# A pinned order for the prologue of a fused transformer layer: row sums among the products of the quarter before, context rows last, extra products in the waits

## The chip, the cores and the metric

The kernel runs on one core of a Trainium2 chip. The number that counts is the device time of one execution in microseconds (us): the median before the change is 1426.35 us over three runs (1426.13, 1426.35 and 1907.31). The names of the engines are those of the profile: PE multiplies matrices, PEld loads its stationary operands, DVE works elementwise and reduces, ACT evaluates functions and copies, POOL is the slow general engine, SP issues the transfers (DMA). TensorE is another name of PE.

## The reference

One layer of a diffusion backbone, in float32: 1024 latent tokens and 256 context tokens of 1024 features. The part that the change touches is the beginning:

```
m_lat = silu(c) @ w_mod + b_mod           # shift and scale of the latent rows
m_ctx = silu(c_ctx) @ w_mod + b_mod       # the same for the context rows
h_lat = rms_norm(x, norm1_g) * (1 + sc1) + sh1
h_ctx = rms_norm(ctx, norm1_g) * (1 + csc1) + csh1
p = h @ w_in                              # 3584 columns, here the 512 of the retention values
```

Behind it come retention and differential attention on the seven column blocks of `w_in`, an output projection, a gated MLP with a depthwise convolution, and a final norm. The change leaves their code alone.

## The kernel before, in words

**Exactness.** Each float32 operand `a` is split into a part `hi`, rounded to a short float format, and the rest `lo = a - hi`. Every product is made in three passes (`passes`, lines 126 to 131): `hi*hi` at line 129, `hi*lo` at line 130, `lo*hi` at line 131, of 128x128 by 128x512 each. A slice of weights is loaded into `raw` (line 186), ACT casts it to `whi` (line 190) and DVE subtracts to `wlo` (line 191).

**The prologue.** It ends where the products `pl` of the next column block begin. The 1024 features are eight slices `d` (or `k`) of 128, taken in four quarters `q` of two slices each. The 1024 latent rows are eight tiles `t` of 128, in two halves. The work is this:

- *Row sums and columns* (`modulation1(q)`, lines 509 to 529). For a quarter, two tiles `wt` of 1 MB of `w_mod` are loaded, and eight products `pr` (line 516) sum them up with `silu(c)`. ACT copies the result to `rw` (line 520), four tiny products `pm` (line 523) turn it into columns, and three small DVE operations (lines 527 and 529) make shift and scale `mcol` of the two slices.
- *First half* (`raw_latents`, lines 566 to 584). A row tile `xt` is squared and summed by ACT (line 533). DVE (line 114) and POOL (line 115) make the factor of its norm, DVE scales the tile (line 535), eight PE transposes `px` (line 579) turn it, and ACT and DVE copy it into `xraw` (lines 582 and 584). `first_latents(q)` applies `mcol` to the two slices of the quarter: DVE at line 589, ACT casts `hi` (line 590), and POOL or DVE subtracts `lo` (line 592, POOL for the odd slice). Then it multiplies the slices with the weights into four running sums `part`, printed as `pn`, one for each row tile.
- *Context rows and second half* (`context_rows`, `latents`). The rows are normed as above, and `modulate` (lines 537 to 548) turns a slice of all of them at once (`pt`, line 541) and makes its `hi` (ACT, line 544), `tmp` (DVE, line 546) and `lo` (line 548, POOL for odd slices). Then come the products of the context's two tiles, `cT`, and of the second half's four tiles, by `natural`.

The value tiles are evacuated by `store_to` (lines 400 to 409), centred and stored.

**What sets the order.** The work is written as generators: `beside(g, rate)` runs a generator next to another loop, which calls `tick()` and so lets the generator go on at that rate. The list of each engine is then set by a scheduler with a model of its own, which moves an instruction ahead of others that wait for operands. Each engine works down its list in order and waits on semaphores. `in_order(start)` ties neighbours of an engine's instructions from a point on in the order in which they are written; before the change it is used only at the end of the kernel. SP issues all loads of the prologue from one queue, in order. The tiles `wt` have four buffers, `xt` five, the weights' `raw` two, and the turned tiles `px`, `pt` and `pm` share three PSUM buffers.

Of the kernel before, what the change touches and what calls it, by code (L numbers as in the profile page):

```python
# [8 lines left out]
F32 = mybir.dt.float32  # L9
# [8 lines left out]
P = 128  # L18
# [42 lines left out]
TAIL = 2  # L61
EARLY = ("S1", "M1", "S0", "M0", "E1", "E0", "R", "C")
# [10 lines left out]
def kernel(  # L73
# [43 lines left out]
    def in_order(start):  # L117
        last = {}
        for ins in nc.cur_bb.bb.instructions[start:]:
            if ins.engine not in FORCE:  # L120
                continue
# [30 lines left out]
    with ExitStack() as p1:  # L152
# [3 lines left out]
        first = ExitStack()  # L156
        xr = first.enter_context(tc.tile_pool(name="xr", bufs=1, side="right"))
# [339 lines left out]
        with ExitStack() as p0:  # L497
# [11 lines left out]
            def modulation1(q):  # L509
                d0 = 2 * q  # L510
                pr = ps_b.tile([P, 512], F32, name="pr", tag="mm")
                for kk in range(2):
                    raw = xp.tile([P, 4, 512], F32, name="wt", bufs=4)
                    nc.sync.dma_start(out=raw, in_=w_mod[q][:, 4 * kk : 4 * kk + 4, :])
                    for j in range(4):
                        mm(pr[32 * j : 32 * j + 32, :], wide[:, 4 * kk + j, :], raw[:, j, :], start=(kk == 0), stop=(kk == 1), tile_position=(0, 32 * j), skip_group_check=True)
                    for j in range(4):
                        tick()
                rw = xp.tile([P, 512], F32, name="rw", bufs=1)
                nc.scalar.copy(rw, pr)  # L520
# [29 lines left out]
            def latents():  # L550
                xs = []
                for t in range(4, 8):
                    xt = xp.tile([P, D], F32, name="xt", bufs=5)
                    nc.sync.dma_start(out=xt, in_=x[t * P : (t + 1) * P, :])
                    normalize(xt, 2 + t)
                    xs.append(xt)
                    yield
                for d in range(KD):
                    modulate(xs, d, 0, hT[0][1][:, d, :], hT[1][1][:, d, :])
                    yield  # L560
# [5 lines left out]
            def raw_latents():  # L566
                xs = []
                for t in range(4):
                    xs.append(xp.tile([P, D], F32, name="xt", bufs=5))
                    nc.sync.dma_start(out=xs[t], in_=x[t * P : (t + 1) * P, :])  # L570
                yield
                for t, xt in enumerate(xs):
                    normalize(xt, 2 + t)
                    for g in range(2):
                        yield
# [915 lines left out]
```

## Time and profile before

| | |
|---|---|
| time, median of three runs | 1426.35 us |
| the profiled execution's own time | 1426.36 us |
| its span | 1424.6 us |
| PE busy | 1372.8 us, 96% of the span |
| first product `pr` of the prologue | 7.05 us |
| first product `pn` of the values | 24.58 us |
| first product `pl` of the next block | 107.72 us |

The profile page has busy times of each engine. A view by windows splits these into stretches of the span, and `PEclk` in it is the granted clock of PE (1.00 is full). The timeline lists one engine's instructions: start, the time from the first one's start to the last one's end, engine, line, operation, result and operands, count, and in brackets the idle time before them with what ended it. Matmuls overlap in it, so the step from one start to the next, and not the length printed, is what one costs. A float32 product that isn't split shows as two records.

### The profile page before, as it was taken

What the parts mean: (1) busy time and instruction counts of PE and PEld (TensorE: products, weight loads), DVE (VectorE), ACT (ScalarE), POOL (GpSimd) and SP (SyncE); (2) the same over time, 40 slices, a digit from 0 to 9 for tenths busy, and PEclk for the clock granted to TensorE, in tenths of its full rate; (3) what the DMA queues carried; (4) which work ended last, traced back from release to release, by engine and by line L of the source; (5) the groups of instructions that cost most, each with busy time, mean ns of one, the idle gap of its engine ahead of it and who ended that gap; (6) DMA issues with size and microseconds to landing.
All of it is one profiled execution on the core that took longest, in us unless ns stands there. A gap on an engine that the chain in (4) does not pass through costs nothing.

```text
span 1424.6 us, 19441 instructions
## 1 busy us (share of the span) xinstructions
PE 1372.8 (96%) x6924; PEld 1141.5 (80%) x6924; DVE 1009.1 (71%) x1503; ACT 735.3 (52%) x1402; POOL 358.9 (25%) x467
## 2 busy tenths in 40 slices
PE   6899999999999899999999999999999999999997
PEld 3578878878887789999888778888888888788886
DVE  3578855533467699888346897788877777898756
ACT  3535623212455688998225665445555545455433
POOL 1230000031777332421201133322222330034003
PEclk8999999999999999999999999999999999999999
DMA  8448874376458378461411223323322235953434
GB/s 321 172 151 303 297 257 144 126 250 189 138 174 203 123 184 184 107 130 60 163 67 74 84 86 112 108 99 111 111 91 82 102 111 177 386 209 107 134 97 148
DMA packets 106953, 219.87 MB, mean 154 GB/s; under 512 B 8868, under 2 KB 47268, under 8 KB 104936
## 3 DMA queue, kind: packets, MB, share of 16 engines
q1 hardware_dynamic: 98728, 193.72, 39.8%
q0 software_dynamic: 8128, 24.91, 7.9%
q8 instruction: 55, 0.90, 0.3%
q14 instruction: 42, 0.34, 0.1%
HBM read 161.18 MB, written 57.41 MB: 153 GB/s over the span
## 4 chain that ended last, share of the span: by engine, by line
PE 44%; issue 3%; DMA 2%; DVE 2%; ACT 1%; POOL 0%; POOLq 0%; DVEq 0%; ACTq 0%
PE chain L129 5%; PE chain L130 5%; PE chain L131 5%; PE c L131 4%; PE c L130 4%; PE c L129 4%; PE third L131 2%; PE third L130 2%; PE third L129 2%; PE po L131 2%; PE po L130 2%; PE po L129 2%; DMA W<-w_down 1%; PE second L130 1%; PE second L131 1%
## 5 line engine op out<-in xcount | busy, mean ns | idle before, releaser
L129 PE MATMUL chain<-T,whi 128*128 128x512 f32 x264 | 103.7, 393 | 5.9 <-ACT ub L1176 3.2
L129 PE MATMUL pl<-hT,whi 128*128 128x512 f32 x256 | 106.5, 416 | 0.0
L130 PE MATMUL chain<-T,whi 128*128 128x512 f32 x264 | 103.5, 392 | 0.0
L131 PE MATMUL chain<-T,wlo 128*128 128x512 f32 x264 | 103.2, 392 | 0.0
L131 PE MATMUL pl<-hT,wlo 128*128 128x512 f32 x256 | 100.6, 393 | 0.0
L130 PE MATMUL pl<-hT,whi 128*128 128x512 f32 x256 | 100.4, 392 | 0.0
L769 DVE TENSOR_REDUCE mt<-pA 128x1 f32<-128x1280 f32 x64 | 95.4, 1490 | 4.1 <-PE pA L766 3.6
L766 PE MATMUL pA<-ks,qhl 128*128 128x512 f32 (+1 forms) x384 | 89.5, 369 | 3.6 <-ACT p L773 3.6
L131 PE MATMUL c<-whi,ghl 128*128 128x512 f32 x232 | 90.4, 390 | 0.8 <-DVE ghl L1252 0.8
L1081 POOL TENSOR_TENSOR cmb<-wrb 128x512 f32<-128x512 f32 x20 | 27.3, 1363 | 250.8 <-DMA wrb<-w_up 156.9
L129 PE MATMUL c<-whi,ghl 128*128 128x512 f32 x232 | 90.3, 389 | 0.0
L130 PE MATMUL c<-wlo,ghl 128*128 128x512 f32 x232 | 90.3, 389 | 0.0
L129 PE MATMUL pn<-whi,hT 128*128 128x512 f32 x192 | 84.5, 441 | 3.7 <-ACT hT L590 3.7
L773 ACT ACTIVATE p<-pA,mt 128x1280 f32<-128x1280 f32 x64 | 85.4, 1335 | 2.4 <-DVE mt L769 2.4
L425 ACT ACTIVATE xb<-pl 32x512 f32<-32x512 f32 (+1 forms) x96 | 56.7, 590 | 52.9 <-PE pl L131 28.6
L932 ACT CAST whi<-cmb 128x512 fp32r<-128x512 f32 x62 | 38.6, 623 | 87.3 <-PE chain L130 65.3
L766 PEld LDWEIGHTS pA<-ks,qhl 128*128 128x128 f32 x384 | 67.6, 189 | 15.6 <-ACT p L773 4.3
L131 PE MATMUL pn<-whi,hT 128*128 128x512 f32 x192 | 76.4, 401 | 0.8 <-POOL hT L548 0.4
L798 PE MATMUL pv<-va,aT 128*128 128x128 f32 x640 | 77.0, 276 | 0.1
L130 PE MATMUL pn<-wlo,hT 128*128 128x512 f32 x192 | 77.0, 403 | 0.0
L798 PEld LDWEIGHTS pv<-va,aT 128*128 128x128 f32 x640 | 74.0, 192 | 0.7 <-DVE yT L827 0.3
L933 DVE TENSOR_TENSOR wlo<-cmb,whi 128x512 fp32r<-128x512 f32 x62 | 57.1, 924 | 21.9 <-ACT whi L932 21.9
(320 smaller groups left out, 3887.0 us busy)
## 6 DMA issues: line engine op xcount, KB each, us to landing
raw<-w_in SPq DMA_DIRECT2D x32, 512.0 KB, 4.8
wm<-w_mod SPq DMA_DIRECT2D x32, 512.0 KB, 4.7
wra<-w_up SPq DMA_DIRECT2D x24, 512.0 KB, 3.4
wrb<-w_up SPq DMA_DIRECT2D x23, 512.0 KB, 3.5
W<-w_down SPq DMA_DIRECT2D x44, 256.0 KB, 6.8
ad<-s SPq DMA_DIRECT2D x20, 512.0 KB, 3.5
wra<-ad SPq DMA_DIRECT2D x20, 512.0 KB, 3.4
wrb<-ad SPq DMA_DIRECT2D x18, 512.0 KB, 4.0
```

Of the source, the lines that this page charges most:

```text
L129: mm(ps, lh, rh, start=first, stop=False, skip_group_check=more)
L130: mm(ps, lh, rl, start=False, stop=False, skip_group_check=more)
L131: mm(ps, ll, rh, start=False, stop=last, skip_group_check=more)
L425: nc.scalar.activation(xb[q * blk : (q + 1) * blk, :], pt[o : o + blk, :], AF.Copy, scale=scale)
L766: mm(self.pa[m][:, c0:c1], self.q[:, i, m, qs], self.k[:, m, c0:c1], start=(i == 0), stop=(i == 1))
L769: nc.vector.tensor_reduce(out=self.mt[:, m : m + 1], in_=self.pa[m][:, :LK], axis=AX.X, op=ALU.min)
L773: nc.scalar.activation(self.p[m], self.pa[m][:, :LK], AF.Exp, scale=-1.0, bias=self.mt[:, m : m + 1], accum_out=self.s[:, m : m + 1])
L798: mm(self.pv, self.aT[:, c, :], self.v[:, c, :], start=(c == 0), stop=(c == NKT - 1))
L932: nc.scalar.copy(hi, src)
L933: nc.vector.tensor_tensor(out=lo, in0=src, in1=r32(hi), op=ALU.subtract)
L1081: nc.gpsimd.tensor_tensor(out=s1, in0=b1, in1=b2, op=ALU.add)
```

## The change

- All of the first half's loads go first: four `xt`, then `wt` of quarters 0 and 1 with a weight slice behind each pair. The rest follows as buffers come free: `wt` of quarter 2, a weight slice, the four row tiles of the second half, `wt` of quarter 3, a weight slice, the context rows.
- The order of PE and SP from there to the end of the first half's products is pinned as written, by `in_order` with those two engines. ACT, DVE and POOL stay with the scheduler.
- The row sums and columns of quarter `q` stand among the products of quarter `q-1`, and the features of quarter `q` are made while the rest of quarter `q-1` is multiplied.
- The second half is turned between the products of the last two quarters. Its products come next, and the context rows, turned between them, are multiplied last.
- `spare(n)` issues `n` products of a tile of ones with itself into a PSUM tile that nobody reads: 16 at the very start, 2 ahead of the first columns, 4 behind them.

The core of the diff (left out: the renaming of an ExitStack, and the moved bodies of functions that stay the same):

```diff
+SPARE = (16, 2, 4)
...
-    def in_order(start):
+    def in_order(start, engines=FORCE):
         last = {}
         for ins in nc.cur_bb.bb.instructions[start:]:
-            if ins.engine not in FORCE:
+            if ins.engine not in engines:
                 continue
...
-            def modulation1(q):
+            wts, prs = {}, {}
+
+            def weights(q, kk):
+                wts[q, kk] = xp.tile([P, 4, 512], F32, name="wt", bufs=4)
+                nc.sync.dma_start(out=wts[q, kk], in_=w_mod[q][:, 4 * kk : 4 * kk + 4, :])
+
+            def row_sums(q, kk):
+                if kk == 0:
+                    prs[q] = ps_b.tile([P, 512], F32, name="pr", tag="mm")
+                raw = wts.pop((q, kk))
+                for j in range(4):
+                    mm(prs[q][32 * j : 32 * j + 32, :], wide[:, 4 * kk + j, :], raw[:, j, :], start=(kk == 0), stop=(kk == 1), tile_position=(0, 32 * j), skip_group_check=True)
+
+            def columns(q):
                 d0 = 2 * q
...
+            def second_half():
+                rows = [xs[t] for t in range(4, 8)]
+                for t, xt in enumerate(rows):
+                    normalize(xt, 6 + t)
+                for d in range(KD):
+                    modulate(rows, d, 0, hT[0][1][:, d, :], hT[1][1][:, d, :])
+                    yield
+
+            def spare(n):
+                dm = pst.tile([P, 4, P], F32, name="dm", tag="tr")
+                for i in range(n):
+                    mm(dm[:, i % 4, :], ones, ones, start=True, stop=True)
...
-            beside(raw_latents(), 1.5, 1.0)
-            modulation1(0)
+            start = len(nc.cur_bb.bb.instructions)
+            for t in range(4):
+                row(t)
+            for q in range(2):
+                for kk in range(2):
+                    weights(q, kk)
+                more()
+            spare(SPARE[0])
+            raw_rows(0)
+            raw_rows(1)
+            row_sums(0, 0)
+            weights(2, 0)
+            raw_rows(2)
+            raw_rows(3)
+            row_sums(0, 1)
+            weights(2, 1)
             more()
+            for t in range(4, 8):
+                row(t)
+            spare(SPARE[1])
+            columns(0)
+            first_features(0)
+            spare(SPARE[2])
+
+            def values(q, n):
+                for _ in range(n):
+                    next(first[q], None)
+                    if q > 1 and turns[0] is not None:
+                        next(turns[0], None)
+
+            first, turns = [first_values(q) for q in range(4)], [None]
             for q in range(1, 4):
-                beside(first_latents(q - 1), 1.25, 0.0)
-                modulation1(q)
-                beside(iter(()), 0.0)
-                more()
-            todo = first_latents(3)
-            for _ in range(2):
-                next(todo)
-            beside(context_rows(), 1.5, 0.0)
-            for _ in todo:
-                tick()
-            beside(latents(), 0.75, 3.0)
+                values(q - 1, 3 if q == 1 else 1 if q == 2 else 2)
+                for kk in range(2):
+                    row_sums(q, kk)
+                    if q == 1:
+                        weights(3, kk)
+                if q == 1:
+                    more()
+                    xc = []
+                    for t in range(NTC):
+                        xc.append(xp.tile([P, D], F32, name=f"xc{t}"))
+                        nc.sync.dma_start(out=xc[t], in_=ctxt[t * P : (t + 1) * P, :])
+                values(q - 1, 1)
+                columns(q)
+                first_features(q)
+                if q == 3:
+                    turns[0] = second_half()
+                values(q - 1, 9)
+            values(3, 9)
+            for _ in turns[0]:
+                pass
+            in_order(start, (mybir.EngineType.PE, mybir.EngineType.SP))
+            beside(context_rows(), 0.4, 0.0)
+            natural(wget, lat_lhs, range(4, NT), keep_rv)
+            beside(iter(()), 0.0)
             natural(wget, ctx_lhs, range(NTC), store_to(kvg_row(1), center=True))
-            beside(iter(()), 0.0)
-            natural(wget, lat_lhs, range(4, NT), keep_rv)
```

`first_values(q)` yields after each of its eight products of three passes (a row tile and a slice), so `values(q, n)` writes `n` of them.

PE's list at the start of the program, before (px are the transposes of the first half's rows):

```order
L516 MATMUL pr<-wt,wide 32x512 x4
L579 MATMUL px<-ident,xt 128x128 x32
L516 MATMUL pr<-wt,wide 32x512 x4
L523 MATMUL pm<-fold,rw 128x2 x4
L129 MATMUL pn<-whi,hT_171 128x512 x2
L130 MATMUL pn<-wlo,hT_171 128x512 x2
L131 MATMUL pn<-whi,hT_173 128x512 x2
L516 MATMUL pr<-wt,wide 32x512 x4
```

and now (dm are the spare products, hT_171 and hT_173 the `hi` and `lo` of the first half's features):

```order
L607 MATMUL dm<-ones 128x128 x16
L573 MATMUL px<-ident,xt 128x128 x16
L521 MATMUL pr<-wt,wide 32x512 x4
L573 MATMUL px<-ident,xt 128x128 x16
L521 MATMUL pr<-wt,wide 32x512 x4
L607 MATMUL dm<-ones 128x128 x2
L529 MATMUL pm<-fold,rw 128x2 x4
L607 MATMUL dm<-ones 128x128 x4
L130 MATMUL pn<-whi,hT_171 128x512
L131 MATMUL pn<-wlo,hT_171 128x512
L132 MATMUL pn<-whi,hT_173 128x512
L130 MATMUL pn<-whi,hT_171 128x512
```

The first row sums have moved behind half of the transposes, the spare products stand at three places, and the products of the first quarter, which went two tiles at a time through one slice, go pass by pass through both slices of one tile.

SP's list from the start of the program, before:

```order
L514 DMA wt<-w_mod 128x2048
L570 DMA xt<-x 128x1024 x4
L514 DMA wt<-w_mod 128x2048
L186 DMA raw<-w_in 128x1024
L514 DMA wt<-w_mod 128x2048 x2
L186 DMA raw<-w_in 128x1024
L514 DMA wt<-w_mod 128x2048 x2
```

and now:

```order
L560 DMA xt<-x 128x1024 x4
L514 DMA wt<-w_mod 128x2048 x2
L187 DMA raw<-w_in 128x1024
L514 DMA wt<-w_mod 128x2048 x2
L187 DMA raw<-w_in 128x1024
L514 DMA wt<-w_mod 128x2048 x2
```

The first 1 MB of `w_mod` stands behind the four row tiles instead of ahead of them.

ACT's list around the third and fourth quarter, before (sq is the square of a row tile, xc a context tile, rw the copied row sums):

```order
L520 COPY rw<-pr 128x512
L190 CAST whi<-raw 128x1024
L590 CAST hT_171<-xraw 128x512 x2
L520 COPY rw<-pr 128x512
L190 CAST whi<-raw 128x1024
L533 ACTIVATE sq,sm<-xc_494 128x1024
```

and now:

```order
L526 COPY rw<-pr 128x512
L191 CAST whi<-raw 128x1024
L584 CAST hT_171<-xraw 128x512
L539 ACTIVATE sq,sm<-xt 128x1024 x2
L584 CAST hT_171<-xraw 128x512
L539 ACTIVATE sq,sm<-xt 128x1024 x2
L526 COPY rw<-pr 128x512
```

The squares of the second half's rows have moved in between the two casts of the third quarter.

73 lines of the change are left out of this document (24 added, 49 removed).

## The prediction

> **What bounds the kernel now.** First the page:
>
> ```profile
> span 1424.6 us, 19441 instructions
> PE 1372.8 (96%) x6924; PEld 1141.5 (80%) x6924; DVE 1009.1 (71%) x1503; ACT 735.3 (52%) x1402; POOL 358.9 (25%) x467
> ```
>
> PE bounds the whole, with 51.8 us of the span idle. Next the view by windows, cut where the timeline shows the first product of the values (24.58), the first turned context tile (57.24), the first product of the second half (81.41) and the next block (107.72):
>
> ```profile
> 0.00:24.58 24.58, 10.79 (x56) 6.87 (x56) 9.21 (x29) 10.38 (x17) 2.39 (x8) 0.92 0.93 368
> 24.58:57.24 32.66, 29.94 (x145) 18.18 (x145) 10.40 (x24) 9.70 (x15) 4.39 (x4) 0.90 0.66 239
> 57.24:81.41 24.17, 23.06 (x109) 17.51 (x109) 21.73 (x44) 15.59 (x29) 10.85 (x11) 0.93 0.28 89
> 81.41:107.72 26.31, 24.52 (x109) 18.73 (x108) 18.71 (x26) 8.46 (x11) 7.56 (x6) 1.00 0.48 158
> 107.72:140.00 32.28, 32.28 (x189) 28.54 (x188) 27.99 (x64) 17.87 (x39) 0.00 (x0) 1.00 0.89 301
> ```
>
> The columns are PE, PEld, DVE, ACT and POOL busy, granted clock, DMA share, GB/s. PE is idle for 13.79 us up to 24.58, for 5.62 us in the next 83.14 us, and not at all behind 107.72. So the change can reach 19.4 us of waits, and the second thing that the windows show: a clock under 1.00. Narrower windows place it:
>
> ```profile
> 17.50:20.60 3.10, 2.99 (x16) 1.77 (x16) 1.25 (x2) 0.59 (x1) 0.00 (x0) 0.50 1.00 419
> 20.80:24.00 3.20, 1.31 (x12) 0.97 (x8) 1.03 (x5) 1.61 (x3) 0.00 (x0) 1.00 1.04 434
> 24.20:27.40 3.20, 2.82 (x6) 1.82 (x6) 1.87 (x3) 0.95 (x2) 0.60 (x1) 0.50 0.87 314
> 27.40:30.60 3.20, 3.20 (x12) 1.31 (x12) 0.00 (x0) 0.00 (x0) 0.67 (x1) 0.50 0.33 99
> 34.00:38.00 4.00, 3.39 (x23) 2.17 (x22) 2.55 (x6) 1.81 (x4) 0.00 (x0) 1.00 0.81 271
> 58.50:61.60 3.10, 3.10 (x9) 2.26 (x10) 2.50 (x3) 1.58 (x4) 2.31 (x3) 0.51 0.00 0
> ```
>
> The clock goes to half after a stretch in which PE had little to do (20.8 to 24.0) and stays there for 6.4 us of products, then again for 3.1 us. At half speed that costs 3.2 + 1.5 = 4.7 us.
>
> **Part 1, up to the first product.** PE's timeline:
>
> ```profile
> 7.05 1.94 PE L516 MATMUL pr<-wt,wide 128*32 128x512 f32 x8 [7.05 <-DMA wt<-w_mod]
> 11.00 3.29 PE L579 MATMUL px<-ident,xt 128*128 128x128 f32 x16 [2.01 <-DVE sm L114]
> 19.48 1.58 PE L516 MATMUL pr<-wt,wide 128*32 128x512 f32 x8
> 21.77 1.05 PE L523 MATMUL pm<-fold,rw 128*128 128x2 f32 x8 [0.71 <-ACT rw L520]
> 24.58 1.22 PE L129 MATMUL pn<-whi,hT 128*128 128x512 f32 x2 [1.76 <-ACT hT L590]
> 32.50 1.06 PE L516 MATMUL pr<-wt,wide 128*32 128x512 f32 x8
> ```
>
> and what the other engines do for it:
>
> ```profile
> 8.19 1.06 ACT L533 ACTIVATE sq<-xt 128x1024 bf16<-128x1024 f32 x1 [5.14 <-DMA xt<-x]
> 10.19 0.75 DVE L535 TENSOR_SCALAR xt<-xt,sm 128x1024 f32<-128x1024 f32 x1 [0.66 <-POOL sm L115]
> 23.33 0.55 DVE L589 TENSOR_SCALAR xraw<-xraw,mcol 128x512 f32<-128x512 f32 x1
> 25.53 0.54 DVE L589 TENSOR_SCALAR xraw<-xraw,mcol 128x512 f32<-128x512 f32 x1
> 26.11 0.62 ACT L590 CAST hT<-xraw 128x512 fp32r<-128x512 f32 x1 [1.58 <-DVE xraw L589]
> 26.80 1.27 POOL L592 TENSOR_TENSOR hT<-xraw,hT 128x512 fp32r<-128x512 f32 x1 [10.13 <-ACT hT L590]
> ...
> 9.61 0.55 POOL L115 TENSOR_TENSOR sm<-sm,mhalf 128x1 f32<-128x1 f32 x1 [9.17 <-DVE sm L114]
> ```
>
> Loads come at these rates (last column):
>
> ```profile
> 2.00:5.00 3.00, 0.00 (x0) 0.00 (x0) 0.98 (x7) 0.22 (x2) 0.00 (x0) 1.00 0.95 262
> 5.00:10.00 5.00, 1.94 (x8) 0.23 (x8) 0.15 (x1) 1.62 (x3) 0.40 (x1) 1.00 1.00 405
> 10.00:15.00 5.00, 3.29 (x16) 3.05 (x16) 2.78 (x6) 3.46 (x7) 1.26 (x3) 1.00 1.03 429
> ```
>
> By 8.19, when the first row tile is there, 0.79 + 3.19 x 0.405 = 2.08 MB have moved; the tiles that had to land make 1.77 MB (two small ones 0.20, `wt` 1.05, a row tile 0.52), so 0.31 MB of later tiles were on their way. Now the rows go first: row `t` lands when 0.51 + 0.52(t+1) MB have moved, at 5.6, 6.9, 8.2 and 9.5 us; the first `wt` at 3.66 MB, 12.0 us; the second at 14.4. The queue is otherwise the same.
>
> The first scaled row came 2.75 us after its square began (8.19 to 10.94). Now DVE takes the second row's factor first, so about 9.0. The 16 transposes of two rows end near 11.4, and PE waits for `wt` until 12.0. A half of the row sums costs 1.06 us at full clock and 1.94 at half (rows at 32.50 and 7.05). The fourth row is scaled near 14.2 (square, copy and factors queued behind each other); its transposes and the second half of the sums end at 16.3 at full clock, 18.1 at half. Before it was 21.06 (19.48 + 1.58). From there to the first product stay 3.52 us (24.58 - 21.06: copy, columns, scale, cast). First product: 19.8 to 21.6, I take 20.7. **Gain 3.9 us.**
>
> The spare products: a float32 product of this shape steps by 0.22 us at full clock (below), 0.45 at half. Sixteen take 3.6 to 7.2 us; begun before 1.8, they end ahead of the first scaled row (9.0): free; if the rows came 2 us earlier they would cost 2. Two lie in the 0.71 us wait for `rw` (at half clock 0.2 over it), four in the 1.76 us wait for the cast (0.9 to 1.8): free.
>
> ```profile
> 356.41 0.39 PE L284 MATMUL po<-kvgf,sc 128*128 128x128 f32 x2
> 356.64 0.39 PE L285 MATMUL po<-Sb,qq 128*128 128x128 f32 x2
> ```
>
> **Part 2, from the first product to the next block.** Work that has to be done, counted by groups of instructions (`hi*hi` alone: 64 + 16):
>
> ```profile
> L129 PE MATMUL pn<-whi,hT 128*128 128x512 f32 x64 | 27.4, 432 | 3.7 <-ACT hT L590 3.7
> L129 PE MATMUL pn<-whi,cT 128*128 128x512 f32 x16 | 6.7, 420 | 0.0
> ```
>
> and priced by steps of the timeline:
>
> ```profile
> 107.49 0.39 PE L131 MATMUL pn<-whi,hT 128*128 128x512 f32 x1
> 107.72 0.39 PE L129 MATMUL pl<-hT,whi 128*128 128x512 f32 x1
> 79.80 0.63 PE L541 MATMUL pt<-ident,xt 128*128 128x128 f32 x4
> 80.19 0.48 PE L129 MATMUL pn<-whi,cT 128*128 128x512 f32 x1
> ```
>
> 80 products of three passes at a step of 0.23 (107.49 to 107.72): 54.6 us at 0.2275. Six halves of row sums at 1.1: 6.6. Three `pm` at 0.9: 2.7. Eight slices turned, 0.39 and a slower next product: 8 x 0.47; the context's at about half: 8 x 0.22. Together 69.4 us. Before, PE was busy for 77.5; without the half clock's 4.7 that is 72.8, so 3.4 us lie in products broken up by single transposes. The new list keeps four transposes together; I keep 2 of the 3.4.
>
> The waits before (view of waits, from 24 to 108):
>
> ```profile
> PE pn L129 <- ACT hT L590: 3.7, 4, 1.8
> PE pt L541 <- DVE tmp L546: 1.6, 3, 0.8
> PE pt L541 <- DVE xc L535: 1.1, 1, 1.1
> ```
>
> Of the first, 1.8 belongs to part 1. The context's 1.1 and the quarters' 1.9 find cover: with the columns of the next quarter made at `pm`, 4 to 6 products of three (2.8 to 4.1 us) lie between `pm` and the first product that needs them, which comes 1.76 us after `pm` at best. What comes instead, since PE can no longer step round a late operand:
> - First quarter: the sixth pass needs POOL's `lo` of the odd slice, 3.5 us after the first pass (26.80 + 1.27 against 24.58). The five ahead of it last 1.2 to 2.2 us: 2.0 us idle.
> - Third quarter: two squares (1.15 us each) stand between the casts on ACT, and their factors ahead of the odd `lo` on POOL. Counted from `pm`: cast 1.7, squares to 4.0, second factor to 5.6 (each row in turn: 0.55 on POOL, 0.75 on DVE), `lo` to 6.9; PE is there after 6 x 0.69 + 5 x 0.23 = 5.3. 1.6 us idle.
> - Second half: the turned slices wait for `tmp`, which waits for POOL, as before; the scheduler has put second-half products there: 1.4 us.
>
> Together 5.0 instead of 5.6. For the half clock I keep 2.5 us, one stretch of 5, since the waits of the first quarter leave PE as idle as 20.8 to 24.0 did. Sum: 69.4 + 2 + 5.0 + 2.5 = 78.9 against 83.1. **Gain 4.2 us.**
>
> Loads are no new bound: every later `wt` and row tile is issued over 5 us ahead of use, at 429 GB/s. Behind 107.72 nothing moves but the start; the next block's weights wait for buffers that PE frees, so they move too.
>
> Total 3.9 + 4.2 = 8.1 us: 1426.36 - 8.1 = 1418.3 us. The profiled execution's 1426.36 us (its span and 1.8 us around it) is the median within 0.01.
>
> [...] The row 17.50:20.60 held eight transposes and row sums, and the next shows full clock. [...]
>
> **Rivals.**
> - *The clock holds.* With the spare products and dense stages PE is near full from 12 to 21, and a wait of 2 us may not throttle it. First product 19.8, no half clock, one wait shorter: 8.1 + 0.9 + 2.5 + 1 = 12.5, 1413.9 us. For it: from 34.0 to 38.0 PE was idle for 0.6 of 4 us and kept its clock; against: 20.8 to 24.0. [...]
> - *Only the front moves.* The pinned order waits as often in quarters 2 and 4 as in 3 (1.6 us each), and the broken products keep their 3.4: 3.9 + 4.2 - 3.2 - 1.4 = 3.5, 1422.9 us.
> - *Slower.* Waits in each quarter keep the clock at half from the first product to the fourth quarter's columns, 29 us with 24 us of work. That work then costs 12 instead of 2.5 more: 1.4 us slower, 1427.8 us. It decides once 21 us of work run at half clock. For it: 24.2 to 27.4 was 88% busy and did not raise the clock. Against: quarters two and three have dense stretches of over 6 us, and 27.4 to 30.6 sufficed.
> - *Lost behind.* The next block starts earlier but meets transfers at a share of 0.89 and waits: 1426 us. Against: it has no wait now, and its loads move with it.
>
> **Chances.** Forecast 0.48, clock holds 0.22, only the front 0.20, slower 0.06, lost behind 0.04. The range 1412.5 to 1424.5 takes in the first three with some spread, and leaves out the last two and as much again of tails. Two per cent is 28.5 us, about what a measurement of this kernel can tell from no change; waits and half clock together are 24.1 us, so faster than that has 0.01, slower 0.02, within 0.97.
>
> **What would show it.** Right: first product near 20.7, `pl` near 99.6, waits of `pn` for POOL at the first quarter's odd slice (2 us) and the third's (1.6), one half-clock stretch behind the first product. Wrong: `px` late because the rows land later than 9.5; PE waiting for `dm`, `wt` or `raw`; half clock beyond 30 us; a wait behind `pl`.

## The result, and the profile after

The changed kernel took 1417.95 us (median of 4 runs, 1417.41 to 1419.94) beside 1426.35 us of the kernel before (1426.13, 1426.35 and 1428.41): a ratio of 0.9945, 95% interval 0.9926 to 0.9964. A fourth run of the kernel before, at 1907.31 us, was far slower and does not enter the comparison. Two later groups of runs, each with its own runs of the kernel before, gave 0.9949 (0.9925 to 0.9973) and 0.9950 (0.9935 to 0.9964). So it is half a per cent faster, within 2%. The profiled execution took 1418.22 us.

The page of the changed kernel, its first two lines:

```profile
span 1416.5 us, 19532 instructions
PE 1374.7 (97%) x6968; PEld 1146.8 (81%) x6968; DVE 1004.9 (71%) x1503; ACT 735.4 (52%) x1402; POOL 359.6 (25%) x467
```

The view by windows, cut at the first `pn`, the first `pl` and the first `pk` (the transposes in `natural_copy`, which turn the first key tile of the next block):

```profile
0.00:20.33 20.33, 14.85 (x100) 11.78 (x100) 9.06 (x29) 10.37 (x17) 2.86 (x8) 1.00 0.90 355
20.33:97.12 76.79, 72.74 (x360) 53.64 (x361) 49.80 (x93) 34.23 (x54) 20.56 (x20) 0.98 0.54 204
97.12:191.48 94.36, 90.44 (x437) 74.95 (x436) 71.06 (x114) 48.51 (x92) 0.95 (x1) 0.99 0.86 291
191.48:200.00 8.52, 8.52 (x31) 7.02 (x32) 4.32 (x5) 1.36 (x3) 0.00 (x0) 0.70 0.91 266
```

The kernel before, up to its first `pl` and from there to its first `pk`:

```profile
0.00:107.72 107.72, 88.32 (x416) 61.30 (x417) 60.05 (x121) 44.13 (x71) 25.19 (x28) 0.94 0.59 215
107.72:199.79 92.07, 90.13 (x437) 75.17 (x436) 70.78 (x114) 49.03 (x92) 0.95 (x1) 1.00 0.88 295
```

Three things are to be seen. The first product came at 20.33 instead of 24.58. The way from there to the next block took 76.79 us instead of 83.14, so the prologue is 10.60 us shorter (107.72 - 97.12). But the way from the first `pl` to the first `pk` grew from 92.07 to 94.36 us, with the same PE work in it, and behind it the clock is 0.70. The prologue's gain is not the kernel's gain.

PE's timeline of the prologue after, the rows with waits and the row sums:

```profile
9.31 1.09 PE L573 MATMUL px<-ident,xt 128*128 128x128 f32 x8 [2.28 <-DVE xt L541]
12.10 1.07 PE L521 MATMUL pr<-wt,wide 128*32 128x512 f32 x8 [0.43 <-DMA wt<-w_mod]
14.76 1.06 PE L573 MATMUL px<-ident,xt 128*128 128x128 f32 x8 [0.57 <-DVE xt L541]
15.75 1.06 PE L521 MATMUL pr<-wt,wide 128*32 128x512 f32 x8
20.33 0.50 PE L130 MATMUL pn<-whi,hT 128*128 128x512 f32 x1 [0.76 <-ACT hT L584]
22.53 0.80 PE L130 MATMUL pn<-whi,hT 128*128 128x512 f32 x1 [0.60 <-ACT hT L584]
43.48 0.50 PE L132 MATMUL pn<-whi,hT 128*128 128x512 f32 x1 [1.26 <-POOL hT L586]
56.03 0.66 PE L547 MATMUL pt<-ident,xt 128*128 128x128 f32 x4 [1.20 <-DVE tmp L552]
59.05 0.66 PE L547 MATMUL pt<-ident,xt 128*128 128x128 f32 x4 [0.75 <-DVE tmp L552]
```

ACT's squares there, which begin as the rows land:

```profile
5.87 1.06 ACT L539 ACTIVATE sq<-xt 128x1024 bf16<-128x1024 f32 x1 [2.81 <-DMA xt<-x]
7.23 1.06 ACT L539 ACTIVATE sq<-xt 128x1024 bf16<-128x1024 f32 x1 [0.22 <-DMA xt<-x]
8.47 1.06 ACT L539 ACTIVATE sq<-xt 128x1024 bf16<-128x1024 f32 x1
```

And the clock, in two narrow windows of the changed kernel's profile:

```profile
22.50:25.90 3.40, 3.24 (x8) 1.68 (x8) 0.00 (x0) 0.00 (x0) 1.27 (x1) 0.50 1.01 425
189.60:196.40 6.80, 4.92 (x14) 4.08 (x15) 6.20 (x7) 1.17 (x2) 0.00 (x0) 0.51 0.90 256
```

The rows' stage runs at full clock (eight transposes in 1.06 to 1.09 us, half of the row sums in 1.06). Half clock comes once behind the first product, for 3.4 us, and again at the first `pk`, for 6.8 us, where the kernel before had none.

Where the 2.3 us go that the next block lost is on DVE's timeline. After:

```profile
179.19 3.93 DVE L471 SCALAR_TENSOR_TENSOR macc<-wm,csil,macc 128x1024 f32<-128x1024 f32 x3
185.73 2.61 DVE L471 SCALAR_TENSOR_TENSOR macc<-wm,csil,macc 128x1024 f32<-128x1024 f32 x2 [2.61 <-DMA wm<-w_mod]
188.25 0.68 DVE L429 SCALAR_TENSOR_TENSOR xa<-pl,rtab 128x512 f32<-128x512 f32 x1
189.45 1.28 DVE L471 SCALAR_TENSOR_TENSOR macc<-wm,csil,macc 128x1024 f32<-128x1024 f32 x1
190.65 0.68 DVE L431 TENSOR_TENSOR xa<-xa,xb 128x512 f32<-128x512 f32 x1
```

and before:

```profile
188.11 3.92 DVE L470 SCALAR_TENSOR_TENSOR macc<-wm,csil,macc 128x1024 f32<-128x1024 f32 x3
192.82 1.28 DVE L470 SCALAR_TENSOR_TENSOR macc<-wm,csil,macc 128x1024 f32<-128x1024 f32 x1 [0.79 <-DMA wm<-w_mod]
195.36 1.29 DVE L470 SCALAR_TENSOR_TENSOR macc<-wm,csil,macc 128x1024 f32<-128x1024 f32 x1 [1.25 <-DMA wm<-w_mod]
196.56 0.68 DVE L428 SCALAR_TENSOR_TENSOR xa<-pl,rtab 128x512 f32<-128x512 f32 x1
198.96 0.69 DVE L430 TENSOR_TENSOR xa<-xa,xb 128x512 f32<-128x512 f32 x1
```

The rotation of the first key tile (`xa`, three instructions of `rotated`) stands on DVE behind and between sums over `w_mod2` (`macc`), and these wait for their `wm` tiles. There are four groups of eight such sums. Those shown are the third group, `modulation2(2)`, which the scheduler has put ahead of the rotation; the second, `modulation2(1)`, ran from 134.5 to 152.2 us in the changed kernel. Three buffers hold the `wm` tiles, so the fourth tile of a group is issued only when the group's first sum is done (issued at 180.51 after, 189.42 before).

The first sum of the group comes 82.1 us behind `pl` after and 80.4 before: 1.7 of the 2.3 us stand there already. Ahead of the sums ACT casts two slices of `w_in` (and DVE subtracts), and ACT waits for these loads. After, then before:

```profile
175.41 1.06 ACT L191 CAST whi<-raw 128x1024 fp32r<-128x1024 f32 x1 [5.51 <-DMA raw<-w_in]
183.55 1.05 ACT L190 CAST whi<-raw 128x1024 fp32r<-128x1024 f32 x1 [3.44 <-DMA raw<-w_in]
```

That is 78.3 us behind `pl` after and 75.8 before. The other 0.6 us is the longer wait for `wm` (2.61 us against 0.79 + 1.25). PE waits for the rotation, in the views of waits from 100 to 300 us: first after, then before.

```profile
PE pk L442 <- DVE xa L431: 4.3, 2, 3.8
```

```profile
PE pk L441 <- DVE xa L430: 2.3, 2, 1.9
```

The table below is used throughout. Times are the starts of the first PE instruction on a tile, in the profiled execution of each run; `pub` is the first product of the stage that follows, and the half clock is worked out from windows of 1 us between 180 and 215 as twice the sum of (1 - clock).

| kernel (run) | `pn` | `pl` | `pk` | `pub` | `pl` to `pub` | longest wait at a `pk` | half clock there |
|---|---|---|---|---|---|---|---|
| before | 24.58 | 107.7 | 199.8 | 289.3 | 181.6 | 1.9 | 0 |
| changed | 20.33 | 97.1 | 191.5 | 283.5 | 186.4 | 3.8 | 6.8 |
| changed (e5) | 20.29 | 96.2 | 191.7 | 282.9 | 186.7 | 4.0 | 3.4 |
| changed (e12) | 20.46 | 96.4 | 191.3 | 283.1 | 186.7 | 4.0 | 6.8 |
| e1, no spare products | 20.97 | 98.4 | 192.1 | 283.0 | 184.6 | 3.2 | 3.4 |
| e2, order not pinned | 22.26 | 103.1 | 196.3 | 285.9 | 182.8 | 2.8 | 0 |
| e3, changed, sums behind | 20.83 | 98.6 | 188.7 | 281.9 | 183.3 | 1.6 | 0 |
| e11, the same again | 20.08 | 98.4 | 187.7 | 280.1 | 181.7 | 1.2 | 0 |
| e4, before, sums behind | 25.26 | 107.3 | 196.6 | 289.0 | 181.7 | 0.8 | 0 |
| e6, sums behind, odd slice on DVE | 20.66 | 97.8 | 187.5 | 280.1 | 182.3 | 1.8 | 0 |
| e7, changed, few loads | 20.96 | 99.7 | 191.0 | 280.5 | 180.8 | 1.0 | 0 |
| e8, before, few loads | 24.76 | 107.3 | 197.6 | 286.9 | 179.6 | 0.2 | 0 |
| e9, `wt` first | 23.13 | 100.5 | 198.3 | 290.2 | 189.7 | 4.6 | 6.8 |
| e10, context first | 20.36 | 98.0 | 192.0 | 283.8 | 185.8 | 3.0 | 3.4 |

Behind `pub` the kernels are alike. What is left of the span there was 1135.3 us before, 1133.0, 1137.7 and 1133.6 in the three profiles of the changed kernel, and 1133.0 to 1138.2 over all fourteen. So one execution against another carries 2 to 3 us of which the change knows nothing. By `pub` the change is worth 5.8 to 6.4 us, in the prologue 10.6 to 11.5, always against the one profile of the kernel before.

### The profile page after: what moved, and what is told of

The parts are those of the page before. It is cut to its first block, busy times and chain, and to the rows that moved or that the text cites. A ratio compares the mean times of both kernels' runs of the same rounds, so it can differ in the third digit from the quotient of the medians.

```text
span 1416.5 us, 19532 instructions
## 1 busy us (share of the span) xinstructions
PE 1374.7 (97%) x6968; PEld 1146.8 (81%) x6968; DVE 1004.9 (71%) x1503; ACT 735.4 (52%) x1402; POOL 359.6 (25%) x467
## 4 chain that ended last, share of the span: by engine, by line
PE 44%; issue 3%; DVE 2%; DMA 2%; ACT 1%; POOL 0%; POOLq 0%; DVEq 0%; ACTq 0%
PE chain L130 5%; PE chain L131 5%; PE chain L132 5%; PE c L132 4%; PE c L130 4%; PE c L131 4%; PE third L130 2%; PE third L131 2%; PE third L132 2%; PE po L132 2%; PE po L131 2%; PE po L130 2%; DMA W<-w_down 2%; PE second L130 1%; PE second L131 1%
## 5 line engine op out<-in xcount | busy, mean ns | idle before, releaser
L809 PE MATMUL pA<-ks,qhl 128*128 128x512 f32 (+1 forms) x384 | 89.5, 369 | 3.6 <-ACT p L816 3.6
L132 PE MATMUL c<-whi,ghl 128*128 128x512 f32 x232 | 90.4, 390 | 1.1 <-DVE ghl L1295 1.1
L975 ACT CAST whi<-wra 128x512 fp32r<-128x512 f32 x55 | 33.8, 621 | 71.1 <-PE third L131 42.3
```

What stands on the lines that cost most here:

```text
L132: mm(ps, ll, rh, start=False, stop=last, skip_group_check=more)
L809: mm(self.pa[m][:, c0:c1], self.q[:, i, m, qs], self.k[:, m, c0:c1], start=(i == 0), stop=(i == 1))
L975: nc.scalar.copy(hi, src)
```

## The experiments

Two theories of where 4 to 5 us went between `pl` and `pub`. **Loads and DVE's order**: the next block is bound by its transfers; PE comes earlier, but the sums that stand ahead of the first key rotation still wait for their tiles. **Only moved**: waits there are simply what the block has, and what is taken away at one tile comes back at the next. The first two runs ask what in the prologue carries the gain.

### e1: without the spare products

```diff
             def spare(n):
+                return
```

> The changed kernel without its 22 spare products, all else as it is. Theory (they hold the clock up in the rows' stage): the row sums cost 1.9 us a half again instead of 1.06, the first product of the values comes near 21.6 to 22 us instead of 20.33, the half clock lasts longer behind it, the next block starts at 99 to 100 us instead of 97.12, and the execution takes 1420 to 1421 us. Rival (the rows' stage waits for loads and the norm's chain anyway, and the clock rises by itself): first product at 20.3 to 20.6 us, next block at 97 to 97.5, time within 0.5 us of 1418.

Measured: 1422.82 us (10 runs), ratio 0.9968 (0.9950 to 0.9986). PE's timeline:

```profile
9.27 3.68 PE L573 MATMUL px<-ident,xt 128*128 128x128 f32 x16 [9.27 <-DVE xt L541]
12.88 1.66 PE L521 MATMUL pr<-wt,wide 128*32 128x512 f32 x8
20.97 0.80 PE L130 MATMUL pn<-whi,hT 128*128 128x512 f32 x1 [1.76 <-ACT hT L584]
```

Sixteen transposes take 3.68 us instead of two times 1.06 to 1.09: without the spare products the rows' stage begins at half clock. Yet the first product is only 0.5 to 0.7 us later: in the changed kernel PE waits 0.20, 0.43 and 0.57 us for rows and for `wt` in this stage, and in e1 slower work fills these waits. So 20.97 lies between what the two theories expected. By `pub` nothing of it is left (283.0 against 282.9 to 283.5). The interval of the times overlaps with the changed kernel's; a loss of about 3 us in the whole is suggested, not shown.

### e2: the order not pinned

```diff
-            in_order(start, (mybir.EngineType.PE, mybir.EngineType.SP))
```

> The changed kernel with its text as it is, but without the tie that pins PE and SP; the scheduler orders them. Theory (the pin carries the middle of the prologue: whole groups of transposes and products together, columns early): the scheduler breaks the groups up, the stretch from first product to next block is 80 to 83 us instead of 76.8, the execution 1421 to 1424 us. Rival (the order of the loads and of the text carries it, the pin only adds the waits of the first and third quarter): next block at 96 to 97.5 us, 1416.5 to 1418.5 us.

Measured: 1425.65 us (10 runs), ratio 0.9991 (0.9977 to 1.0006): no difference from the kernel before, and above the 1421 to 1424 expected. The stretch to `pl` took 80.8 us, as the theory had it. The first product comes 1.8 to 2.0 us later than in the changed kernel and `pl` 6.0 to 6.9 us later; PE's waits from 24 to 104 us hold one for the context row that the pinned order does not have:

```profile
PE pn L132 <- POOL hT L586: 1.9, 3, 1.2
PE pt L547 <- DVE xc L541: 1.8, 1, 1.8
PE pn L130 <- ACT hT L584: 1.1, 2, 0.7
```

So the pinned order carries more than half of the prologue's gain. And of these 6 to 7 us only 2.4 to 3.0 are left at `pub`: from `pl` on, e2 takes 182.8 us and the changed kernel 186.4 to 186.7. That speaks for a limit there that does not move with PE.

### e3 and e4: the sums behind the first key rotation, in both kernels

The same edit in the changed kernel (e3) and in the kernel before (e4): a dependency without a semaphore that puts the first `macc` sum of `modulation2(1)` behind the first rotation on DVE. `then` is called in `transposed` once the first tile is rotated.

```diff
-        modulation2(1)
-        transposed(wg, [q[:, 1] for q in rqk_d], rtab, 64, RET_SCALE, 0, by_head[:5], True)
+        def sums_behind():
+            start = len(nc.cur_bb.bb.instructions)
+            first = [i for i in nc.cur_bb.bb.instructions if i.engine == mybir.EngineType.DVE][-1]
+            modulation2(1)
+            ins = next(i for i in nc.cur_bb.bb.instructions[start:] if i.engine == mybir.EngineType.DVE)
+            tc.add_manual_dep(ins, first.name, ...)
+
+        transposed(wg, [q[:, 1] for q in rqk_d], rtab, 64, RET_SCALE, 0, by_head[:5], True, sums_behind)
```

> The changed kernel with one more tie, far behind the prologue: the eight sums of the second modulation row on DVE (macc) come behind the first rotated tile of the key block instead of ahead of it. Theory (the prologue's gain is partly given back there: PE waits 3.84 us for the rotated tile, because DVE first waits for the sums' loads, and then runs 5 us at half clock): the wait and the half clock go, 3.8 + 2.1 = 5.9 us, and 1412 to 1414 us are left. Rival (the loads bound that stretch, so that the wait comes back at the next tiles): PE waits as long in sum between 185 and 260 us, and the time stays within 1 us of 1418.

> The kernel before the change, with the same tie of the sums behind the first rotated tile. Theory: its wait there was 1.94 us with the clock at full, so it gains 1.9 us, 1424.4 us; against it the changed kernel with the same tie then shows the prologue's whole gain, 10.6 us. Rival (the place has nothing to do with the prologue's gain): both kernels gain the same by the tie, and stay 8 us apart.

The tie holds back more than the group that it names: with the `wm` tiles in three buffers, `modulation2(2)` comes behind the rotation too (in e3 all sums from 187.3 us on).

Measured: e3 1416.48 us (4 runs), ratio 0.9926 (0.9907 to 0.9945); e4 1426.86 us (10 runs), ratio 1.0000 (0.9989 to 1.0011). The `pk` on PE's timeline in e3, with the waits ahead of each:

```profile
188.71 0.60 PE L442 MATMUL pk<-ident,xa 128*128 128x128 f32 x4
196.62 0.66 PE L442 MATMUL pk<-ident,xa 128*128 128x128 f32 x4 [0.93 <-DVE xa L431]
202.55 0.66 PE L442 MATMUL pk<-ident,xa 128*128 128x128 f32 x4 [0.25 <-DVE xa L431]
```

The wait at the first `pk` is gone, in both kernels, and waits at the next ones take its place: 2.8 us in 3 in e3, 2.0 in 4 in e4 (2.3 before). e3's time lies between the 1412 to 1414 us of the first theory and the second's 1417 to 1419. That waits come back is the second theory, and in the kernel before it is all: nothing was gained, where about 1.9 us were expected. But in the changed kernel one wait of 3.8 to 4.0 us became several of at most 1.6, and the half clock of 3.4 to 6.8 us is gone with it: `pl` to `pub` takes 183.3 us (181.7 in e11) instead of 186.4 to 186.7. What the edit saves is wait and clock in about equal parts: from `pl` to `pub` PE's idle time falls from 4.4 us to 3.1 (2.2 in e11), and its busy time, which half clock makes longer, from 181.9 us to 180.2 (179.5).

### e5 and e6: the changed kernel again, and with an odd slice on DVE besides

e5 is the changed kernel itself. e6 is e3 with one more edit, against the third quarter's wait at 43.48:

```diff
-                    eng = nc.gpsimd if d % 2 else nc.vector
+                    eng = nc.gpsimd if d % 2 and d != 5 else nc.vector
```

> The changed kernel itself again, beside the three others of this group, so that they can be read against it. Both theories: within 0.1% of 1418 us; the first `pl` at 97 to 98 us, the first `pk` at 191 to 192 us after a wait of 3 to 5 us, and the clock at 0.50 for some 6 us around it, since the same wait must come back if it belongs to the kernel and not to the one execution.

> Changed kernel with two ties: the first `macc` sum of the next block behind the first key rotation on DVE, and the low part of slice 5 of the third quarter on DVE instead of GpSimd, whose wait was 1.26 us at 43.5 us. Theory (PE's waits are simply time): the third quarter's wait falls to about 0.3 us, `pl` starts 1 us earlier than in the run with the first tie alone (98.56 us there), so about 97.5, the first `pk` waits under 1.5 us, and the time is 1.5 to 3.5 us below the changed kernel's. Rival (the waits are only moved on): DVE, which now has one subtraction more, is late for the fourth quarter by the same microsecond, and the waits behind the first `pk` add up to the changed kernel's 4.3 us again: within 1 us of the changed kernel.

Measured: e5 1420.68 us (6 runs), ratio 0.9949 (0.9925 to 0.9973), the wait at the first `pk` again 4.0 us, with 3.4 us of half clock instead of the 6 expected. So the wait belongs to the kernel. The time was 2.7 us above 1418, outside the 0.1% expected, and `pl` came at 96.2, ahead of the 97 to 98 expected. e6 1417.48 us (5 runs), ratio 0.9929 (0.9905 to 0.9953). In its third quarter:

```profile
44.05 0.50 PE L132 MATMUL pn<-whi,hT 128*128 128x512 f32 x1 [1.43 <-DVE sm L115]
```

The wait for GpSimd became one of 1.43 us for DVE, put down there to the factor `sm` of a second-half row, which DVE also has to make: close to the rival, which expected the delay a quarter later. `pl` came at 97.8, near the theory's 97.5, but with 3.4 us of half clock behind the first product where e3 had 6.8, so the edit need not have done it. The rest of e6 is e3's gain.

### e7 and e8: half of the loads of that block, in both kernels

```diff
-                wt = m2p.tile([P, D], F32, name="wm2", bufs=3)
-                nc.sync.dma_start(out=wt, in_=w_mod2[i, k])
+                if i != 1 or k % 2 == 0:
+                    wt = m2p.tile([P, D], F32, name="wm2", bufs=3)
+                    nc.sync.dma_start(out=wt, in_=w_mod2[i, k])
```

> Changed kernel in which the sum over `w_mod2` of the block ahead of the first `pk` loads only every second tile `wm` and uses it twice (half of that part of the weights is left out, so its modulation is not the reference's; 4 loads of 0.5 MB go, and all products stay). Theory (the transfers of 100 to 190 us set the moment at which DVE gets to the key rotation): the `macc` waits for `wm` go, the first `pk` waits under 1.5 us, no half clock around it, and the way from the first `pl` to the first `pub` falls from 186.4 to 181 to 184 us. Rival (DVE's order alone makes the wait, or the raw tiles of `w_in` do, which land late ahead of these loads): the first `pk` still waits over 3 us.

> Kernel before with the same halving of the `wm` loads of that block (the same part of the weights left out). Theory (before, the transfers were just in time, with waits of 0.79 and 1.25 us for `wm` that cost PE about 2 us at the first `pk`): its `pk` waits fall from 2.3 us in all to under 1, and the way from the first `pl` to the first `pub` falls from 181.6 by 1 to 2 us. With the other kernel of this pair this gives what the prologue alone is worth where the loads leave room: 9 to 11 us. Rival: no change within the 2 to 3 us by which such stretches differ between runs.

The loads left out are those of `modulation2(1)`, at 130 to 155 us, and not those of the sums that stand right ahead of the rotation. The edit thus takes 2 MB out of the queue 30 us earlier and leaves the later loads as they are.

Measured in one execution each: 1416.49 and 1423.09 us. The waits at `pk`, e7 and then e8:

```profile
PE pk L442 <- DVE xa L431: 1.3, 2, 1.0
```

```profile
PE pk L441 <- DVE xa L430: 0.2, 1, 0.2
```

and the first sum of the third group in e7:

```profile
179.66 3.92 DVE L472 SCALAR_TENSOR_TENSOR macc<-wm,csil,macc 128x1024 f32<-128x1024 f32 x3
```

All sums stand where they stood on DVE, and 2 MB of transfers fewer take 2.8 of the 3.8 us of wait away. The waits for `wm` were expected to go; they only fell, from 2.61 to 1.70 us; the larger part came from the slices of `w_in`, so that the first sum stands 79.9 us behind `pl` instead of 82.1. These are the raw tiles that the rival named, though the wait of over 3 us that it expected did not stay. `pl` to `pub` falls by 5.6 to 5.9 us in the changed kernel (to 180.8; 181 to 184 was expected) and by 2.0 in the kernel before (to 179.6). Of the 4.8 to 5.1 us by which the changed kernel was slower on this way than the kernel before, 1.2 are left. So transfers make the wait, and DVE's order is how it reaches PE. That their sum over the whole way does it is not shown: see e10.

The pair's own difference at `pub` is 6.4 us, not the expected 9 to 11. Here the reason lies in the prologue: in this execution e7 reached `pl` only at 99.7, with 6.8 us of half clock behind the first product against none in e5 and e12, which reached it at 96.2 and 96.4. With their prologue, and if the block moved along with it, the pair would be 9.7 to 9.9 us apart; that sum is an argument, no measurement.

### e9 and e10: the order of the loads, and the context's place

```diff
+            weights(0, 0)
             for t in range(4):
                 row(t)
             for q in range(2):
                 for kk in range(2):
-                    weights(q, kk)
+                    if q + kk:
+                        weights(q, kk)
```

e10 calls `natural(wget, lat_lhs, range(4, NT), keep_rv)` behind the context's products instead of ahead of them.

> Changed kernel with the first `wt` load again ahead of the four row tiles, as before the change. Theory (the rows' landings set the front): 1.05 MB at 0.41 MB per us puts every row 2.5 us later (squares on ACT from 8.2 instead of 5.87), the last rows are turned about 2 us later, and the first `pn` comes at 21.5 to 22.5 us instead of 20.33; so the order of the loads carries 1 to 2 of the 4.25 us of the front. Rival (the chain of squares, factors and scalings behind the landings sets it): the first `pn` comes at 20.8 or earlier.

> Changed kernel with the context's products ahead of the second half's instead of behind them. Theory (only the waits of the turned slices for `tmp`, 1.9 us, can move): the context's 11 us of products cover them, and the first `pl` comes 1 to 2 us earlier than in a run of the changed kernel with as much half clock. Rival (context last is worth something): the context's own operands are late there, PE waits over 1 us for them, and `pl` comes as late or later.

Measured in one execution each: e9 1425.04 us, the first product at 23.13, later than the expected 21.5 to 22.5. PE's timeline:

```profile
11.16 3.68 PE L573 MATMUL px<-ident,xt 128*128 128x128 f32 x16 [3.89 <-DVE sm L115]
14.77 1.74 PE L521 MATMUL pr<-wt,wide 128*32 128x512 f32 x8
23.13 0.49 PE L130 MATMUL pn<-whi,hT 128*128 128x512 f32 x1 [0.76 <-ACT hT L584]
```

The landings do set the front, and a second effect comes to it: the spare products end at 7.27, PE is idle for 3.89 us instead of 2.28, and the rows' stage runs at half clock. Both together make the order of the loads worth 2.7 to 2.8 us at the first product, two thirds of that part's gain. Behind `pl` e9 lost more than any other kernel (189.7 us to `pub`): besides the 4.6 us at the first `pk` PE waited 1.4 and 0.9 us for weights. Its transfers ran at 281 GB/s there, and by the first `pk`, at 198.3, they had moved 50.4 MB (228 GB/s for 100.5 us, 281 for 97.8), as much as in the two kernels of the study by theirs. Why it took longer is open.

e10 reached `pl` at 98.0, 1.6 to 1.8 us later than the two profiles of the changed kernel that had as little half clock (none): the rival, with a smaller wait than it named. The waits of `pt` for `tmp` stayed at 1.9 us, since those transposes stand ahead of both groups of products; new are two of 0.3 us for the context's own tiles, and PE is busy with the 48 products of the context for 12.56 us instead of the 11.04 in e12, broken up by single transposes. Context last is worth 1 to 2 us, in one execution.

e10 also bears on the transfers behind `pl`. There 25.3 MB had moved by `pl`, 2.4 more than in the changed kernel, so that only 25.2 were left up to `pk` (258 GB/s for 98.0 us, 268 for 94.0), about as in e7 (25.5). Yet the way took 94.0 us and the first `pk` waited 3.0, where e7 waited 1.0. The first sum of the group stood 80.5 us behind `pl`, but then the sums waited 3.25 and 0.63 us for `wm`. So the bytes of the whole way do not set the wait by themselves; it goes by when single loads land.

### e11 and e12: the changed kernel with and without the tie, on one chip

> The changed kernel with the first `macc` sum of the next block tied behind the first key rotation on DVE, again, now beside the changed kernel itself on the same chip. Theory (the order on DVE turned the prologue's gain into 4 us of wait and half clock, of which the tie brings back about half): 1 to 3 us below the changed kernel of this group. Rival (the waits come back at the next tiles): within 1 us of it.

> The changed kernel as it is, as the measure for the run with the tie. Both theories: a ratio to the kernel before of 0.993 to 0.997; the first `pk` after a wait of 3 to 5 us; `pl` between 96 and 100 us, the later the longer the clock stays at half behind the first product (none in one execution, 3 us in the first).

Measured: e11 1417.77 us (6 runs, 1414.52 to 1421.81), ratio 0.9940 (0.9920 to 0.9960); e12 1419.08 us (6 runs, 1416.04 to 1422.13), ratio 0.9950 (0.9935 to 0.9964). The difference of 1.3 us lies where it was expected, but the intervals overlap. What the profiles show is the stretch: `pl` to `pub` 5.0 us shorter with the tie, no half clock in it; over all profiles 181.7 to 183.3 with it (e3, e6, e11) and 186.4 to 186.7 without.

## Why the prediction came out as it did

1418.3 us was forecast, 1417.95 measured, and 1419.1 to 1420.7 in the later groups: inside the range, and within the two per cent that had 0.97. The sum of 8.1 us, though, came from two parts that were too small and one that was missing; the medians give 5.7 to 8.4 us, the landmarks up to `pub` 5.8 to 6.4. That the first group came within 0.4 us of the forecast is luck. In the two profiled executions the gains of 4.25 and 6.35 us less the 4.8 lost behind `pl` make 5.8, and 2.3 us more come from behind `pub`, where executions differ by more than that.

- *Part 1, up to the first product: right.* 20.7 forecast, 20.29 to 20.46 measured in three profiles. The squares began at 5.87, 7.23 and 8.47, behind landings forecast for 5.6, 6.9 and 8.2; `wt` at 12.10 against 12.0; the end of the row sums at 16.8 against 16.3 to 18.1. e9 confirms that the loads' order carries it. The spare products were free, as said. With them the rows' stage ran at full clock in the three profiles of the changed kernel (eight transposes in 1.06 to 1.09 us), without them sixteen took 3.68 (e1); but in e3, e6 and e7, which have them too, the clock was half for 3.4 us of this stage. By them the first product gained only 0.5 to 0.7 us.
- *The work of part 2: right.* 69.4 us and 2 for broken products, 71.4. In e12, at full clock throughout, PE was busy for 71.42 of the 75.94 us from first product to `pl`; the pinned order is what brings it there (e2).

```profile
20.46:96.40 75.94, 71.42 (x361) 52.86 (x362) 49.83 (x93) 34.27 (x54) 20.56 (x20) 1.00 0.55 206
```

- *The waits of part 2: 5.0 forecast, 4.05 measured* (76.79 - 72.74; 4.5 in e5 and e12). The second half waited 1.95 instead of 1.4, the third quarter 1.26 instead of 1.6. The first quarter cost 0.6 behind its first pass and, where the clock held, 0.6 at the sixth, together 1.2 instead of 2.0: e12 shows the sixth pass at 24.00, 3.54 us behind the first, just as reckoned, but the five passes ahead of it, themselves held up by the second cast, filled more of the time.
- *The half clock of part 2: one stretch, but smaller.* 3.4 us instead of 5 in the first profile, none in e5 and e12, up to 6.8 in other kernels' executions with the same order. "The clock holds" was true of this stage in two of three executions. The price was also lower than half of the time: from the first product to `pl` it took 75.9 us without it, 76.8 with 3.4 us, and 77.4 to 78.8 with 6.8 (e1, e3, e11, e7). That is 0.9 us for the first 3.4 and 1.5 to 2.9 for 6.8, since PE has waits in it anyway. Together the gain of part 2 was 6.35 us, and 7.2 in the executions without half clock, where 4.2 was forecast.
- *"Behind 107.72 nothing moves but the start": wrong, the step that failed.* The rival "lost behind" had the mechanism, with a chance of 0.04, and all of the gain lost; what came was 4.8 to 5.1 us of 10.6 to 11.5. The forecast took PE's full window from 107.72 to 140.00 as proof that the block had no wait, and did not follow it to its first `pk`, where the trace of before had 1.9 us of wait for DVE behind sums that waited for `wm`. Nor was "its loads move with it" so: at the first `pk`, 23.16 + 27.16 = 50.3 MB had moved before (215 GB/s for 107.72 us, 295 for 92.07), 22.92 + 27.46 = 50.4 MB after, though PE had reached `pl` 10.6 us earlier. The loads up to that point are the same in both kernels, and after the change the way there took 94.4 us, where PE's work is 90.4. Of the 4.8 us, 2.3 are the longer way to `pk`, 1.9 of it wait, and 2.5 the half clock behind it (`pk` to `pub` 92.0 against 89.5).
- *Why the wait is longer after:* settled in part. e7 shows that the transfers make it, and the traces show where: at the slices of `w_in`. The first of them was issued at the same place (70.3 us behind `pl` after, 71.0 before), but its cast came 8.0 us after that instead of 4.9. The DMA engines were busy for 0.95 of the time between in both kernels and moved 2.7 MB instead of 1.4, so more lay ahead of it: the 1 MB of `rtab` and three smaller transfers had been issued in the 4.8 us up to it, against 7.7 us before. In e5 and e12 the two numbers are 4.8 us and 7.4 to 7.6, in e7 6.4 and 5.7. This is read from traces; no run moved these transfers apart.
- *The clock and the transposes:* the changed kernel's rows' stage, transposes and row sums in turn, ran at full clock (eight transposes in 1.06 to 1.09 us). e2 is the plainest case: between 9.55 and 15.54 PE did nothing but transposes, and the clock came back within them (0.50 from 11 to 14 us, 0.83 from 14 to 15, 1.00 from 15 on).

```profile
10.84 3.79 PE L573 MATMUL px<-ident,xt 128*128 128x128 f32 x16 [0.20 <-DVE sm L115]
15.09 0.52 PE L573 MATMUL px<-ident,xt 128*128 128x128 f32 x3 [0.45 <-DVE xt L541]
15.54 1.07 PE L521 MATMUL pr<-wt,wide 128*32 128x512 f32 x8
```

Sixteen take 0.237 us each there, the next three 0.17, and the row sums behind them their full-clock time.

- *What would show it wrong* named "a wait behind `pl`", and that is how it was found.

## What to carry to other kernels

A stage that starts earlier brings its gain only as far as the next limit that does not start earlier with it (10.6 to 11.5 us in the prologue were 5.8 to 6.4 at `pub`): before a forecast says "nothing moves but the start", follow the next stage on every engine to PE's first wait. The bytes moved up to that wait are a first sign (50.3 and 50.4 MB here); they are not enough, as e10 shows, and the loads that the wait ends on have to be followed one by one. Look in the next block for work that waits for transfers and stands, on an engine's list, ahead of something PE needs, as the sums stood here, with 2.61 us of wait for `wm`, ahead of `xa`. Moving it behind may only move the wait; here one wait of 3.8 to 4.0 us came with 3.4 to 6.8 us of half clock, and 2.8 us in three pieces (e3) with none. The next thing to try here, which was not tried, is to bring those of the block's loads forward that are late, `rtab` and the slices of `w_in`: the DMA engines of the changed kernel stand nearly idle in the prologue's middle. Other loads did not do it: e10 had moved 2.4 MB more by `pl`, and its first `pk` still waited 3.0 us.

```profile
46.00:52.00 6.00, 6.00 (x40) 4.95 (x39) 5.08 (x11) 4.82 (x8) 0.61 (x2) 1.00 0.19 57
52.00:60.00 8.00, 6.05 (x35) 4.49 (x33) 6.55 (x9) 5.82 (x10) 5.00 (x5) 1.00 0.06 24
60.00:70.00 10.00, 10.00 (x45) 8.26 (x44) 8.81 (x17) 2.93 (x5) 3.65 (x3) 1.00 0.19 58
```

## What was not expected of the hardware

- *Half clock came in pieces of 3.4 us.* Between 180 and 215 us it lasted 0, 3.4 or 6.8 us in all fourteen profiles (3.40 to 3.42 and 6.84 as worked out from the windows), and there it went with the length of one wait: none for longest waits of 0.2 to 2.8 us (eight profiles), 3.4 us for 3.0 and 3.2, 3.4 or 6.8 for 3.8 to 4.6. The length of the wait does not settle it alone: 4.0 us came with 3.4 in e5 and with 6.8 in e12. What sets the length of a piece is not shown.
- *In the prologue it came without such a wait.* From 12.5 to 22.5 us the changed kernel's longest wait is 0.76 us, and up to there PE's starts agree within 0.2 us in its three profiles; then one ran at half clock for 3.4 us and two did not. In the rows' stage the wait behind the spare products was 2.06 us in e7, and the sixteen transposes behind it took 3.43 us; with 2.28 to 2.61 us in the three profiles of the changed kernel they ran at full clock. What decides there is open.
- *In e1 the clock column said 1.00 while PE ran at half.* It shows full clock for 9.3 to 12.7 us, while sixteen transposes take 3.68 us, as in e9, where the column shows 0.50 from 10 to 16 us. There the durations tell, not the column.
